# A two-layer decoder trunk: six more pairs of gate blocks and the third SwiGLU's later up blocks as seven half products, and compressed scores as three products per pair of heads

## The chip, the cores and the metric

The kernel runs on one core of a Trainium2 chip. The metric is the device time of one execution in microseconds (us). Three runs of the kernel before took 2000.01, 2000.32 and 2001.31 us; their median is 2000.32.

## The reference

The input is one sequence of 512 tokens with 1024 features, in float32. Two macaron layers follow each other; each adds half a SwiGLU, a mixer and half a second SwiGLU to the stream. The first mixer is an mLSTM. After it one shared set of keys and values is made, among them 31 compressed keys per key head. The second mixer is sparse attention with 16 query heads and 4 key heads; one of its three branches scores each query against the compressed keys.

```python
def swiglu(h, w_in, w_out):
    a, b = jnp.split(h @ w_in, 2, axis=-1)
    return (jax.nn.silu(a) * b) @ w_out
# in a layer, four times in all (D_MODEL = 1024, D_FF = 2816):
h = h + 0.5 * swiglu(rmsnorm(h, g), w_in, w_out)
# in nsa_mixer, per block of 64 queries:
s_c = jnp.einsum('bqhgd,bchd->bqhgc', qq, k_cmp)
p_c = masked_softmax(s_c, ...)
```

## The kernel before

The stream is kept transposed: eight tiles `h` of 128 features x 512 tokens. Every float32 factor of a product is split into a rounded part `hi` and the rest `lo`, and a product of two is three matmuls, hi·hi, lo·hi and hi·lo (`mm3`, L216 to L220). All matmuls are issued at L214. A split is one ScalarE copy (`hi`, L223) and one VectorE subtraction (`lo`, L224); for plain weight blocks the same two stand at L158 and L159.

**Stages.** They run in this order: `ffn0`, `mlstm`, `ffn1`, `kv`, `ffn2`, `nsa`, `ffn3`. The last steps of `kv` (the compressed keys and values, `compress`) are woven into the start of `ffn2`, the third SwiGLU.

**A SwiGLU** (`ffn`, from L337) has 22 gate blocks and 22 up blocks of 128 columns. A plain block multiplies its eight weight strips with the eight tiles of x: 24 matmuls with 512 columns. The blocks run in groups. After a group, its gated products `ghi`, `glo` are multiplied with the group's rows of `w_out` into the eight blocks of the output, two blocks at a time, and each is added to `h`. A group whose product still lacks the norm's factor r is folded: the output is multiplied with r in one VectorE instruction (L515) and added with a second (L516). In the last group r is multiplied into the up block (L362) instead, and the output needs one (L512).

**By seven.** In SwiGLUs 0, 1 and 3 (`SEVEN`) the up blocks from the third on are computed in pairs: with the features cut in two, the tokens cut in two and two blocks of columns, a pair is a 2x2 product of halves, which is done with seven products (Winograd's form of Strassen's method) where eight would do. `by_seven` (L389) issues 7 products x 4 strips x 3 = 84 matmuls with 256 columns. The price is paid elsewhere. Four quarters of the two weight blocks are fetched (`fetch`, L164), VectorE makes four sums of them (`add_quarters`, L173), seven quarters are split (`load_forms`), `x_forms` (L374) makes the sums of x once per SwiGLU, and five VectorE instructions and one ScalarE copy put the results together (L412 to L432). The list `GATES` names the pairs of gate blocks that go the same way: 6, 8, 10, 12, 14, 16 and 20. The groups are 0 to 7, 8 to 15 and 16 to 21 (`EVENS`). In `ffn2` every block is plain, and its groups are 0 to 7, 8 to 14 and 15 to 21 (`THIRDS`).

**The order of the loads.** A dry pass writes down every weight in the order of use; `load_weight` then works that list ahead of the use: up to `ahead` weights (2, or 3 in `SEVEN`) beyond the one wanted. A `fetch` or an `add` in the list is done when the list reaches it. Four buffers hold split weights (`whi`, `wlo`), two hold raw ones. Loads are issued by SyncE, in order. Within the dependencies the framework's scheduler decides each engine's order.

**Scores against compressed keys.** `project_q(b)` makes the queries of two heads, 64 rows each. For each head ScalarE and VectorE write hi and lo into one half of a tile of 128 rows (L1014, L1015) and SyncE copies them to the other half (L1017): four DMAs per pair. A compressed key tile holds hi in its upper and lo in its lower 64 rows, so a head's scores are two matmuls per 128 tokens; `compressed(b)` issues 4 x 2 x 2 = 16 with 32 columns.

Of the kernel before, what the change touches and what calls it, by code (L numbers as in the profile page):

```python
# [19 lines left out]
P = 128  # L20
# [11 lines left out]
GATES = (6, 8, 10, 12, 14, 16, 20)  # L32
# [64 lines left out]
class Net:  # L97
    def __init__(self, ctx, tc, a, order=None):
# [11 lines left out]
        self.fp = None  # L110
        self.ahead = 2
# [51 lines left out]
    def fetch(self, *at):  # L163
# [9 lines left out]
    def add_quarters(self, *at):  # L173

        q = self.raws[at]
        s = self.sums[at] = [None] + [self.fp.tile([P, 512], F32, name=f"s{j}", tag=f"s{j}", bufs=1) for j in range(1, 5)]
# [160 lines left out]
    def ffn(self, i, r=None):  # L337
        nc, tc = self.nc, self.tc
        seven = i in SEVEN
        self.ahead = 3 if seven else 2  # L340
        TT, STT = nc.vector.tensor_tensor, nc.vector.scalar_tensor_tensor
        N = T // 2
        with ExitStack() as ctx:
            pp = ctx.enter_context(tc.tile_pool(name=f"fps{i}", bufs=8 if seven else 6, space=PSUM, reuse_waits="tile"))
            gp = ctx.enter_context(tc.tile_pool(name=f"fg{i}", bufs=8, reuse_waits="tile"))
            self.fp = gp

            nc.vector.memset(gp.tile([P, 96], F32, name="home", tag="home", bufs=1)[:, :1], 0.0)
# [9 lines left out]
            def gate(t, u):  # L358

                if k1 == FB:  # L360
                    v = gp.tile([P, T], F32, name="fd", tag="fd", bufs=2)
                    TT(v, u, r, op=ALU.mult)  # L362
                    u = v
                TT(t, t, u, op=ALU.mult)
                hi = gp.tile([P, T], F32R, name="ghi", tag="ghi")
                lo = gp.tile([P, T], F32R, name="glo", tag="glo")
# [6 lines left out]
            def x_forms(k):  # L373
# [4 lines left out]
                one, two = (gp.tile([P, 3 * N], F32, name="fw", tag="fw", bufs=2) for _ in range(2))  # L378
# [11 lines left out]

            def by_seven(p):
# [35 lines left out]
                TT(two(u1), W[:, :2, :], two(Z), op=ALU.add)  # L427
# [41 lines left out]
            for k0, k1 in EVENS if seven else THIRDS:  # L469
                gs = []  # L470
                for p in range(k0, k1, 2) if seven else range(k0, k1):
                    if seven and p:
                        if p in GATES:
                            ts = [silu(t) for t in (yield from by_seven(p))]
                        else:
                            ts = []
                            for j in range(2):
                                w = self.weight("ffn_in", i, p + j)
                                pa = ps_mm()
# [15 lines left out]
                for m in range(0, KB, 2):  # L495
# [8 lines left out]
                    for k, j in order:  # L504
                        self.mm3(po[j], self.strip(w2[j], k), gs[k], k == 0, k == n - 1)
                        yield
# [851 lines left out]
```

## Time and profile before

One execution was profiled: it took 2000.02 us, its span (first to last instruction) is 1998.2 us.

| engine | busy, us | share of the span |
|---|---|---|
| PE (matmuls) | 1984.4 | 99% |
| PEld (weight loads) | 1715.8 | 86% |
| DVE (VectorE) | 1462.7 | 73% |
| ACT (ScalarE) | 954.4 | 48% |
| POOL (GpSimd) | 166.0 | 8% |

PE is TensorE; its matmuls overlap one another, so a matmul's own duration is longer than the distance to the next one, and what a matmul costs is read from the distance of their starts. L214 is line 214 of the kernel; a name such as `pmm<-xhi,whi` gives the output tile and the inputs. The granted clock of TensorE was full (1.0) in all slices.

### The profile page before, as it was taken

Reading aid. Unit: us, or ns where it says so; the run is one execution under the profiler, and the core shown is the slowest. Engines: PE = TensorE matmul, PEld = TensorE weight load, DVE = VectorE, ACT = ScalarE, POOL = GpSimd, SP = SyncE. Lnnn points to the kernel's source line nnn. Section 1 sums busy time; section 2 is a strip of 40 time slices with the busy share of each in tenths; the row PEclk is TensorE's granted clock in tenths of the full one; section 3 lists DMA queues with packets and bytes.
Section 4 is the critical chain, followed back from the end, with each engine's and each line's share of the span. In section 5 each row is a group of like instructions: output and inputs, shape, how many; then the busy total and the mean of one; then the engine's idle time right before and its main releaser. Section 6 shows DMA issues by size and latency. Waiting matters only on the chain.

```text
span 1998.2 us, 29540 instructions
## 1 busy us (share of the span) xinstructions
PE 1984.4 (99%) x11330; PEld 1715.8 (86%) x11330; DVE 1462.7 (73%) x2604; ACT 954.4 (48%) x1752; POOL 166.0 (8%) x216
## 2 busy tenths in 40 slices
PE   9999999999999999999999999999999999999999
PEld 7989999788778999898888888888778778999898
DVE  8959878757897789686656544445788888769785
ACT  6425334445654345254444322234888865435242
POOL 0000000012200000000101000001444420000000
PEclk9999999999999999999999999999999999999999
DMA  5423422323232323313334332323121132323322
GB/s 189 121 89 103 125 75 65 115 83 95 64 122 90 114 78 111 100 54 116 105 108 123 110 98 87 111 89 105 44 54 43 43 101 80 110 85 101 112 63 90
DMA packets 71469, 188.46 MB, mean 94 GB/s; under 512 B 8480, under 2 KB 9376, under 8 KB 71328
## 3 DMA queue, kind: packets, MB, share of 16 engines
q1 hardware_dynamic: 69936, 183.82, 30.6%
q8 instruction: 89, 1.46, 0.3%
q10 hardware_dynamic: 1008, 1.70, 0.2%
q0 software_dynamic: 384, 1.05, 0.2%
q14 instruction: 52, 0.43, 0.1%
HBM read 177.10 MB, written 2.10 MB: 90 GB/s over the span
## 4 chain that ended last, share of the span: by engine, by line
PE 91%; DVE 3%; ACT 3%; DMA 2%; issue 1%; POOL 0%; SPq 0%; DVEq 0%; ACTq 0%; POOLq 0%
PE pmm L214 80%; PE S L214 3%; PE po L214 2%; PE vps L214 2%; PE pt L1129 1%; DMA q<-in_ffn_in 1%; PE paux L214 1%; ACT pr L1097 1%; PE pn L214 1%; DVE wlo L159 0%; DMA wraw<-in_ffn_in 0%; ACT pth L223 0%; PE pt L214 0%; PE dm L214 0%; PE pg L214 0%
## 5 line engine op out<-in xcount | busy, mean ns | idle before, releaser
L214 PE MATMUL pmm<-xhi,whi 128*128 128x512 f32 (+2 forms) x1468 | 512.2, 349 | 1.4 <-DVE h L1167 0.9
L214 PE MATMUL pmm<-xhi,wlo 128*128 128x512 f32 (+2 forms) x1468 | 508.5, 347 | 0.9 <-DVE wlo L159 0.9
L214 PE MATMUL pmm<-xlo,whi 128*128 128x512 f32 (+2 forms) x1468 | 508.4, 346 | 0.7 <-DVE xlo L267 0.5
L158 ACT ACTIVATE whi<-wraw 128x1024 fp32r<-128x1024 f32 (+3 forms) x296 | 252.1, 867 | 480.4 <-PE pmm L214 360.4
L159 DVE TENSOR_TENSOR wlo<-wraw,whi 128x1024 fp32r<-128x1024 f32 (+3 forms) x296 | 296.4, 1012 | 68.9 <-ACT whi L158 66.0
L214 PEld LDWEIGHTS pmm<-xhi,wlo 128*128 128x128 f32 (+1 forms) x1468 | 277.7, 189 | 34.9 <-DVE wlo L159 1.3
L214 PEld LDWEIGHTS pmm<-xhi,whi 128*128 128x128 f32 (+1 forms) x1468 | 278.0, 189 | 33.0 <-ACT xhi L266 1.6
L214 PEld LDWEIGHTS pmm<-xlo,whi 128*128 128x128 f32 (+1 forms) x1468 | 278.0, 189 | 32.4 <-DVE xlo L267 2.1
L214 PE MATMUL pmm<-ghi,whi 128*128 128x512 f32 x704 | 274.2, 389 | 0.0
L214 PE MATMUL pmm<-glo,whi 128*128 128x512 f32 x704 | 274.0, 389 | 0.0
L214 PE MATMUL pmm<-ghi,wlo 128*128 128x512 f32 x704 | 273.9, 389 | 0.0
L214 PE MATMUL pmm<-thi,whi 128*128 128x256 f32 x816 | 230.9, 283 | 0.0
L214 PE MATMUL pmm<-tlo,whi 128*128 128x256 f32 x816 | 230.9, 283 | 0.0
L214 PE MATMUL pmm<-thi,wlo 128*128 128x256 f32 x816 | 230.9, 283 | 0.0
L223 ACT ACTIVATE whi<-s 128x512 fp32r<-128x512 f32 x204 | 123.0, 626 | 175.1 <-PE pmm L214 112.1
L214 PEld LDWEIGHTS pmm<-thi,whi 128*128 128x128 f32 x816 | 156.7, 192 | 0.0
L214 PEld LDWEIGHTS pmm<-tlo,whi 128*128 128x128 f32 x816 | 156.7, 192 | 0.0
L214 PEld LDWEIGHTS pmm<-thi,wlo 128*128 128x128 f32 x816 | 156.7, 192 | 0.0
L223 ACT ACTIVATE whi<-q 128x512 fp32r<-128x512 f32 x153 | 95.9, 627 | 125.4 <-PE pmm L214 96.1
L214 PEld LDWEIGHTS pmm<-ghi,wlo 128*128 128x128 f32 x704 | 132.1, 188 | 27.5
L214 PEld LDWEIGHTS pmm<-ghi,whi 128*128 128x128 f32 x704 | 132.2, 188 | 27.2
L214 PEld LDWEIGHTS pmm<-glo,whi 128*128 128x128 f32 x704 | 132.2, 188 | 27.1
(341 smaller groups left out, 3120.9 us busy)
## 6 DMA issues: line engine op xcount, KB each, us to landing
q<-in_ffn_in SPq DMA_DIRECT2D x204, 256.0 KB, 2.8
wraw<-in_ffn_in SPq DMA_DIRECT2D x73, 512.0 KB, 3.6
wraw<-in_ffn_out SPq DMA_DIRECT2D x56, 512.0 KB, 3.6
wraw<-in_ffn_out SPq DMA_DIRECT2D x24, 384.0 KB, 3.1
wraw<-in_ffn_out SPq DMA_DIRECT2D x16, 448.0 KB, 3.4
wraw<-in_m_qk SPq DMA_DIRECT2D x8, 512.0 KB, 3.6
wraw<-in_m_v SPq DMA_DIRECT2D x8, 512.0 KB, 3.5
wraw<-in_m_og SPq DMA_DIRECT2D x8, 512.0 KB, 3.6
```

Source lines behind the costliest of these rows:

```text
L158: nc.scalar.activation(hi[:p, c], raw[:p, c], AF.Copy)
L159: nc.vector.tensor_tensor(lo[:p, c], raw[:p, c], hi[:p, c].bitcast(F32), op=ALU.subtract)
L214: self.nc.tensor.matmul(out, lhsT, rhs, start=start, stop=stop)
L223: self.nc.scalar.activation(hi, src, AF.Copy)
L1097: nc.scalar.activation(s, S[:, i, :n], AF.Exp, bias=nx[:, i:i + 1], scale=cc, accum_out=z[:, i:i + 1])
L1129: nc.tensor.transpose(pt[:, col:col + P], pr[br][:, ROW[tb] + sb * P:ROW[tb] + sb * P + P], self.ident)
```

## The change

- `GATES` becomes 4, 6, 8, 10, 12, 14, 16, 18, 20: in SwiGLUs 0, 1 and 3 the pairs 4 and 18 of gate blocks go by seven too.
- The third SwiGLU (`ffn2`) has four groups, 0 to 7, 8 to 11, 12 to 15 and 16 to 21 (`LATER`). In the last three the gate blocks stay plain and the up blocks go by seven. Only the first group is folded; the others multiply r into the up block. The sums of x are made by a new `x_forms_late`, from the tiles of x, in the second half of the first group's output product. The tiles come from pools opened where `compress` had its own; before block 8 the SwiGLU's pool of tiles is closed and another opened (`room`). Quarters and one of the sums have a single buffer there (`qbufs`), `W` too.
- In `by_seven` the first result u1 stays in `W`, and the third sum of quarters overwrites the quarter q[2,1].
- The compressed keys are two tiles, hi and lo, with the two heads of a pair side by side as 2 x 32 columns, each in its own 64 rows with zeros in the others. `project_q` splits both heads' queries at once (`N[b]`), `compressed` issues 4 x 3 = 12 matmuls with 64 columns, and SyncE fills all four head tiles from `N[b]`: eight DMAs per pair.

```diff
-GATES = (6, 8, 10, 12, 14, 16, 20)
+GATES = (4, 6, 8, 10, 12, 14, 16, 18, 20)
+
+LATER = ((0, 8), (8, 12), (12, 16), (16, 22))
...
-                t = q[a, b] = self.fp.tile([P, 512], F32, name=f"q{a}{b}", tag=f"q{a}{b}", bufs=2)
+                t = q[a, b] = self.fp.tile([P, 512], F32, name=f"q{a}{b}", tag=f"q{a}{b}", bufs=self.qbufs)
...
+        s = self.sums[at] = {j: self.fp.tile([P, 512], F32, name=f"s{j}", tag=f"s{j}", bufs=1) for j in (1, 2, 4)}
+        s[3] = q[2, 1]
...
+        self.qbufs = 2 if seven else 1
...
-                if k1 == FB:
-                    v = gp.tile([P, T], F32, name="fd", tag="fd", bufs=2)
+                if not fold:
+                    v = gp.tile([P, T], F32, name="fd", tag="fd", bufs=2) if i == 2 and not k0 else u
                     TT(v, u, r, op=ALU.mult)
...
+            def x_forms_late(k):
+
+                one = sums.tile([P, T], F32, name="tw", tag="tw", bufs=1)
+                two = sums.tile([P, 3 * N], F32, name="tv", tag="tv", bufs=1)
+                (hi1, lo1), (hi2, lo2) = ([t.bitcast(F32) for t in x[b]] for b in (k, k + 4))
+                c = [two[:, N * j:N * j + N] for j in range(3)]
+                TT(one, hi1, lo1, op=ALU.add)
+
+                TT(one[:, :N], one[:, N:], one[:, :N], op=ALU.subtract)
+                for t, half, other in (c[0], slice(N, T), one[:, :N]), (c[1], slice(N, T), one[:, N:]), (c[2], slice(N), c[0]):
+                    TT(t, hi2[:, half], other, op=ALU.subtract)
+                    TT(t, t, lo2[:, half], op=ALU.add)
+                hi = tp.tile([P, 4 * N], F32R, name="thi", tag="thi", bufs=4)
+                lo = tp.tile([P, 4 * N], F32R, name="tlo", tag="tlo", bufs=4)
+                self.split(one[:, :N], hi[:, :N], lo[:, :N])
+                self.split(two, hi[:, N:], lo[:, N:])
+                xt.append((hi, lo))
...
-                W = gp.tile([P, 3, N], F32, name="fw", tag="fw", bufs=2)
+                W = gp.tile([P, 3, N], F32, name="fw", tag="fw", bufs=1 if i == 2 else 3)
-                u1, u2 = (gp.tile([P, T], F32, name="fu", tag="fu", bufs=4) for _ in range(2))
+                u1, u2 = W[:, :2, :].rearrange("p c n -> p (c n)"), gp.tile([P, T], F32, name="fu", tag="fu", bufs=self.qbufs)
...
-            for k0, k1 in EVENS if seven else THIRDS:
-                gs = []
-                for p in range(k0, k1, 2) if seven else range(k0, k1):
-                    if seven and p:
-                        if p in GATES:
+            for k0, k1 in EVENS if seven else LATER:
+                gs, fold = [], k1 < FB if seven else not k0
+                if not seven and k0 == LATER[1][0]:
+                    brief.close()
+                    room("fg2b", 32)
+                    self.ahead = 3
+                for p in range(k0, k1, 2) if seven or k0 else range(k0, k1):
+                    if p and (seven or k0):
+                        if seven and p in GATES:
                             ts = [silu(t) for t in (yield from by_seven(p))]
                         else:
                             ts = []
                             for j in range(2):
+                                if not seven and j == 0 and p != LATER[1][0]:
+                                    self.plan("fetch", i, FB + p)
                                 w = self.weight("ffn_in", i, p + j)
+                                if not seven and (j == 0) == (p != LATER[1][0]):
+                                    if j:
+                                        self.plan("fetch", i, FB + p)
+                                    self.plan("add", i, FB + p)
...
+                        if not seven and not k0 and m >= 4 and t % 8 == 0:
...
+                            x_forms_late((m - 4) + t // 8)
                         self.mm3(po[j], self.strip(w2[j], k), gs[k], k == 0, k == n - 1)
...
+                N[b] = hi, lo = [mp.tile([P, T], F32R, name=n, tag="qn", bufs=3) for n in ("nh", "nl")]
+                self.split(qs, hi, lo)
                 for j in range(2):
-                    s, e = slice(64 * j, 64 * j + 64), slice(64 - 64 * j, 128 - 64 * j)
-                    hi = mp.tile([P, T], F32R, name="qh", tag="q", bufs=8)
-                    lo = mp.tile([P, T], F32R, name="ql", tag="q", bufs=8)
-                    nc.scalar.activation(hi[s], qs[s], AF.Copy)
-                    TT(lo[s], qs[s], hi[s].bitcast(F32), op=ALU.subtract)
-                    for t in (hi, lo):
-                        nc.sync.dma_start(t[e].bitcast(F32), t[s].bitcast(F32))
-                    Q[2 * b + j] = (hi, lo)
+                    Q[2 * b + j] = [mp.tile([P, T], F32R, name=n, tag="q", bufs=8) for n in ("qh", "ql")]
+                    for t, n in zip(Q[2 * b + j], N[b]):
+                        for e in range(2):
+                            nc.sync.dma_start(t[64 * e:64 * e + 64].bitcast(F32), n[64 * j:64 * j + 64].bitcast(F32))
...
-                    for j in range(2):
-                        for part in range(2):
-                            self.mm(Sc[:, tb, j, :], Q[2 * b + j][part][:, tb * P:(tb + 1) * P], self.KC[:, b // 2, :],
-                                    tb + j + part == 0, False)
+                    for n, part in enumerate(((0, 0), (1, 0), (0, 1))):
+                        self.mm(Sc[:, tb].rearrange("p h c -> p (h c)"), N[b][part[0]][:, tb * P:(tb + 1) * P],
+                                self.KC[part[1]][:, b // 2].rearrange("p h c -> p (h c)"), tb + n == 0, False)
```

## Rows read from the trace of the kernel before

**Rows 1.** The page: its first line, the busy time of the engines, and the granted clock of TensorE in 40 slices.

```profile
span 1998.2 us, 29540 instructions
PE 1984.4 (99%) x11330; PEld 1715.8 (86%) x11330; DVE 1462.7 (73%) x2604; ACT 954.4 (48%) x1752; POOL 166.0 (8%) x216
...
PEclk9999999999999999999999999999999999999999
```

**Rows 2.** Busy time of each engine in stretches: most of SwiGLU 0, the end of the third SwiGLU's first output product, the 11 us after it, the rest of the third SwiGLU, the attention.

```profile
core 0: us, PE busy (x) PEld busy (x) DVE busy (x) ACT busy (x) POOL busy (x), PEclk, DMA share, GB/s
33.00:341.00 308.00, 308.00 (x2035) 284.47 (x2034) 253.82 (x419) 136.78 (x220) 2.09 (x2) 1.00 0.31 94
1122.00:1156.00 34.00, 34.00 (x152) 28.14 (x151) 20.13 (x25) 9.25 (x10) 0.00 (x0) 1.00 0.38 113
1156.00:1167.00 11.00, 11.00 (x50) 9.13 (x49) 4.44 (x5) 2.65 (x3) 0.00 (x0) 1.00 0.36 114
1156.00:1397.00 241.00, 241.00 (x1069) 198.09 (x1068) 113.42 (x147) 74.44 (x94) 6.08 (x6) 1.00 0.32 97
1397.00:1622.00 225.00, 222.28 (x1384) 177.03 (x1382) 184.13 (x486) 190.63 (x514) 93.06 (x144) 1.00 0.17 45
```

**Rows 3.** Matmuls in order of time (start, duration): the first and the last of 54 in a row with 512 columns, and of 103 in a row with 256.

```profile
99.76 0.39 PE L214 MATMUL pmm<-ghi,whi 128*128 128x512 f32 x1
...
111.78 0.39 PE L214 MATMUL pmm<-ghi,wlo 128*128 128x512 f32 x1
...
79.74 0.28 PE L214 MATMUL pmm<-thi,whi 128*128 128x256 f32 x1
...
91.98 0.28 PE L214 MATMUL pmm<-thi,whi 128*128 128x256 f32 x1
```

**Rows 4.** VectorE in order of time in the third pair by seven of SwiGLU 0's second group, and the first matmul of that pair's up blocks (PE).

```profile
185.68 0.68 DVE L178 TENSOR_TENSOR s<-q,q 128x512 f32<-128x512 f32 x1
186.28 0.68 DVE L180 TENSOR_TENSOR s<-q,q 128x512 f32<-128x512 f32 x1
...
187.49 0.69 DVE L224 TENSOR_TENSOR wlo<-q,whi 128x512 fp32r<-128x512 f32 x1
...
189.29 0.42 DVE L417 TENSOR_TENSOR fq<-pmm,fw 128x256 f32<-128x256 f32 x1
189.62 0.69 DVE L224 TENSOR_TENSOR wlo<-s,whi 128x512 fp32r<-128x512 f32 x1
...
190.96 0.28 PE L214 MATMUL pmm<-xhi,whi 128*128 128x256 f32 x1
```

**Rows 5.** The same one pair later (the fourth and last of the group): the split of the first form of the up blocks, and the matmul that uses it.

```profile
208.71 0.71 DVE L224 TENSOR_TENSOR wlo<-q,whi 128x512 fp32r<-128x512 f32 x1
...
211.12 0.28 PE L214 MATMUL pmm<-xhi,whi 128*128 128x256 f32 x1
```

**Rows 6.** The end of SwiGLU 0's third group: VectorE (in brackets its idle time and what ended it), ScalarE's splits of the last two gated products, the first matmul of the output product and the 26th, which is the first to read the fifth `glo`.

```profile
321.92 0.69 DVE L420 TENSOR_TENSOR fw<-fq,pmm 128x512 f32<-128x512 f32 x1 [0.78 <-PE pmm L214]
...
324.80 0.69 DVE L427 TENSOR_TENSOR fu<-fw,pmm 128x512 f32<-128x512 f32 x1 [0.78 <-PE pmm L214]
...
330.09 1.29 DVE L224 TENSOR_TENSOR glo<-ft,ghi 128x512 fp32r<-128x512 f32 x2
...
328.73 1.24 ACT L223 ACTIVATE ghi<-ft 128x512 fp32r<-128x512 f32 x2 [1.01 <-DVE ft L364]
...
326.04 0.40 PE L214 MATMUL pmm<-ghi,whi 128*128 128x512 f32 x1
...
331.73 0.39 PE L214 MATMUL pmm<-glo,whi 128*128 128x512 f32 x1
```

**Rows 7.** Groups of instructions by shape (count, busy us, mean ns): the largest split of the sums of x in SwiGLUs 0, 1 and 3, and the two instructions that split a plain block of 512 KB.

```profile
L224 DVE TENSOR_TENSOR tlo<-fw,thi 128x768 fp32r<-128x768 f32 x12 | 11.4, 954 | 1.2 <-ACT thi L223 1.2
...
L159 DVE TENSOR_TENSOR wlo<-wraw,whi 128x1024 fp32r<-128x1024 f32 x145 | 179.7, 1240 | 30.5 <-ACT whi L158 29.7
...
L158 ACT ACTIVATE whi<-wraw 128x1024 fp32r<-128x1024 f32 x145 | 153.3, 1060 | 293.3 <-PE pmm L214 212.6 <-DMA wraw<-in_ffn_out 49.0 <-issue 15.4
```

**Rows 8.** DMA issues: line or tile, engine, count, KB each, median us to landing; and the piece of the chain of waits in which the four quarters for the second SwiGLU's first pair arrive.

```profile
q<-in_ffn_in SPq DMA_DIRECT2D x204, 256.0 KB, 2.8
wraw<-in_ffn_in SPq DMA_DIRECT2D x73, 512.0 KB, 3.6
...
569.70 5.64 DMA q<-in_ffn_in
```

**Rows 9.** The attention: two of the matmuls against compressed keys with ten between them, one of SyncE's issues, the first matmul of the first head's own scores, and the groups of the scores and of the half splits.

```profile
1401.39 0.26 PE L214 MATMUL S<-KC,qh 128*128 128x32 f32 x1
...
1402.62 0.26 PE L214 MATMUL S<-KC,ql 128*128 128x32 f32 x1
...
1402.78 0.47 PE L214 MATMUL S<-K,qh 128*128 128x512 f32 x1
...
1396.39 0.55 SPq L1017 DMA_DIRECT2D ql<-ql  x1
...
L214 PE MATMUL S<-KC,ql 128*128 128x32 f32 x64 | 14.4, 256 | 0.0
...
L1015 DVE TENSOR_TENSOR ql<-qs,qh 64x512 fp32r<-64x512 f32 x16 | 11.7, 734 | 0.7 <-ACT qh L1014 0.4
...
L1014 ACT ACTIVATE qh<-qs 64x512 fp32r<-64x512 f32 x16 | 10.1, 631 | 0.2
```

More of the change, by code (lines that the diff above doesn't have):

```diff
@@ L110, in __init__ @@
         self.fp = None
+        self.compressed = False
         self.ahead = 2
@@ L364, in gate @@
                 TT(t, t, u, op=ALU.mult)
-                hi = gp.tile([P, T], F32R, name="ghi", tag="ghi")
-                lo = gp.tile([P, T], F32R, name="glo", tag="glo")
+                bufs = 8 if seven or not k0 else 6
+                hi = gp.tile([P, T], F32R, name="ghi", tag="ghi", bufs=bufs)
+                lo = gp.tile([P, T], F32R, name="glo", tag="glo", bufs=bufs)
                 self.split(t, hi, lo)
@@ L376, in x_forms @@
                 g1, g2 = (self.g[:, G_FFN + i * KB + b:G_FFN + i * KB + b + 1] for b in (k, k + 4))
-                one, two = (gp.tile([P, 3 * N], F32, name="fw", tag="fw", bufs=2) for _ in range(2))
+                one, two = (gp.tile([P, 3 * N], F32, name="fw", tag="fw", bufs=3) for _ in range(2))
                 h2, c = self.h[k + 4], [two[:, N * j:N * j + N] for j in range(3)]
@@ L425, in by_seven @@
                 yield from product(Z[:, :N], a12, 2)
-                TT(two(u1), W[:, :2, :], two(Z), op=ALU.add)
+                TT(W[:, :2, :], W[:, :2, :], two(Z), op=ALU.add)
                 a22 = self.weight("form", i, p, 3)[0]
@@ L503, in ffn @@
                         order.sort()
-                    for k, j in order:
+                    for t, (k, j) in enumerate(order):
+                        if not seven and not k0 and m >= 4 and t % 8 == 0:
+                            if m == 4 and t == 0:
+                                assert self.compressed
+                                right = dict(bufs=1, side="right", reuse_waits="tile")
+                                tp = ctx.enter_context(tc.tile_pool(name="ft2", **right))
+                                brief = ExitStack()
+                                sums = brief.enter_context(tc.tile_pool(name="ft2s", **right))
+                            x_forms_late((m - 4) + t // 8)
                         self.mm3(po[j], self.strip(w2[j], k), gs[k], k == 0, k == n - 1)
@@ L510, in ffn @@
                         for c in (slice(0, T // 2), slice(T // 2, T)) if last else (slice(0, T),):
[L511 removed]
+                            if not fold:
                                 STT(h[:, c], po[j][:, c], 0.5, h[:, c], op0=ALU.mult, op1=ALU.add)
@@ L825, in kv @@
         self.V = [kvp.tile([P, 2 * KVH, 2 * HD], F32R, name=f"V{tb}") for tb in range(NTB)]
-        self.KC = kvp.tile([P, KVH, CW], F32R, name="KC")
+        self.KC = [kvp.tile([P, KVH, 2, CW], F32R, name=f"KC{part}") for part in range(2)]
         self.VC = kvp.tile([P, KVH, 2, 2 * HD], F32R, name="VC")
@@ L911, in compress @@
             late.close()
+            self.compressed = True
         with ExitStack() as ctx:
```

25 lines of the change are left out of this document (16 added, 9 removed).

## The prediction

> **What bounds the kernel now.** I read the page first, then the busy time by stretches, then the order of time of single engines. The page has TensorE (PE) busy for 99% of the span at full granted clock [rows 1]; since matmuls overlap, that alone proves little. The stretches are better: in SwiGLU 0 and in the third SwiGLU PE is busy for every microsecond, with VectorE at 82% in the one and 47% in the other [rows 2]. The order of time settles it. 54 matmuls with 512 columns start (111.78 - 99.76) / 53 = 0.2268 us apart, 103 with 256 columns (91.98 - 79.74) / 102 = 0.1200 us apart [rows 3], and the SwiGLUs run at these distances throughout. There the time is the number of matmuls times their distance, as long as split weights and gated products are ready in time. The attention is different: PE 222 of 225 us, but ScalarE 191 and VectorE 184 [rows 2]; there engines take turns, and a matmul saved is not always a microsecond saved.
>
> **The sum's own time.** The profiled execution took 2000.0 us, 1.8 of it outside the span [rows 1]; the median of the runs, 2000.3, is the same within what follows. A difference under 0.2% (4 us) can't be told from none in this kernel.
>
> **A pair by seven.** Plain, a pair is 2 x 24 = 48 matmuls x 0.2268 = 10.88 us; by seven it is 84 x 0.1200 = 10.08. That saves 0.80 us. The change makes 6 more such pairs in SwiGLUs 0, 1 and 3 (4 and 18 in each) and 7 in the third: 13 x 0.80 = 10.4 us of matmuls, 4.8 in the three and 5.6 in the third. The output products keep their 528 matmuls, however the groups are cut, since the group sizes add up to 22 blocks either way.
>
> The Trainium skill, in "TensorE: Matmul & The Clock Gate" (Back-to-back issue gap), gives an isolated matmul N / 2.4 + 2.5 ns: 216 ns with 512 columns and 109 with 256. By that a pair would save 48 x 0.2158 - 84 x 0.1092 = 1.19 us, and the 13 pairs 15.4, which would bring the forecast below to 1985.8. The rows lie 11 ns above it at both sizes; the sum goes by the rows.
>
> **SwiGLUs 0, 1 and 3: VectorE.** Back to back its 512-column instructions start 0.60 us apart (186.28 - 185.68) and a 256-column one takes 0.33 (189.62 - 189.29) [rows 4]. One unit by seven needs 4 sums + 7 splits (6.6 us) and 2 x 0.60 + 3 x 0.33 (2.2) to put results together: 8.8. A gate and an up unit, with two silu factors and two gates (2 x 0.60 + 4 x 0.60), make 21.2 us against 20.16 of PE. So in a row of such pairs VectorE falls back 1.1 us per pair. The trace shows it: the first form of the up blocks is ready 190.96 - 188.18 = 2.78 us ahead of its matmul in the second group's third pair [rows 4], and 211.12 - 209.42 = 1.70 in the fourth [rows 5]. Group two is not changed. The first group gets two such pairs in a row, fewer than the four that group two stands. The third group gets three, 16, 18 and 20, and there r is multiplied in too, 2 x 0.60 per pair. Lead in its last pair: the 2.78 of group two's third pair less 2 x 1.2 = 0.4 us. Still positive. At the end of that group the fifth `glo` now is ready at 330.09 + 0.69 = 330.78, 0.95 us before its matmul at 331.73, and VectorE waited for PE twice for 0.78 us in the last unit [rows 6]. The extra pair costs it 1.1 + 1.2 = 2.3; 1.56 of that goes into these waits, 0.74 into the 0.95. Nothing is left to lose, so I take 0.3 us per SwiGLU; the bounds are 0 and 2.3. Net: 4.8 - 0.9 = 3.9 us. Keeping u1 in `W` and the third sum in a quarter moves no work; the second makes one sum wait for another on the same engine.
>
> **The third SwiGLU.** 5.6 us come off PE. Three things are new.
>
> First, `x_forms_late`: per tile pair one add of 0.60, seven of 0.33, and splits of 0.33 and 0.95 [rows 4, 7], 4.2 us, so 17 for four. Then four sums (2.4) and two splits (1.2) before the first unit by seven: 20.5 us of VectorE. It idles 34.0 - 20.1 = 13.9 us in the stretch before block 8 and 11.0 - 4.4 = 6.6 in its two plain blocks, 20.4 in all [rows 2]. That just fits if the scheduler draws the sums forward. If it keeps them to the last 22 us of the output product, about a third of the 13.9 is lost. I take 1.0 us, bounds 0 and 4.
>
> Second, groups of four. In the third group of SwiGLU 0 the fifth `ghi` is ready at 328.73 + 0.62, 3.3 us after the output product's first matmul at 326.04, and the `glo` at 4.7 [rows 6]. With six blocks the matmul wants it at 5.7. With four blocks the last two products are the third and the fourth, wanted after 12 and 13 matmuls, 2.7 and 2.9 us. PE so waits 0.6 us (the `ghi` alone) to 1.8 (the `glo` in the same chain), unless the scheduler lets later matmuls pass. VectorE is less busy here than there, so I take 1.0 for each of two groups, 2.0 us; bounds 0 and 3.6.
>
> Third, single buffers. A pair's quarters can be fetched only when the previous unit's last form is split, which waits for a weight buffer until that unit begins. What hides it is the unit itself, 10.08 us: the last split is done about 1.4 us into it (0.6 and 0.7 on the two engines [rows 4, 9]), the last quarter takes 2.8 and the next plain block's 512 KB, behind it on SyncE, 3.6 [rows 8]: 7.8, and its two splits 1.06 + 1.24 [rows 7]: 10.1. That is just in time, with three quarters loaded earlier, and with slack if the scheduler issues the block's load, which has little to wait for, ahead of the last quarter. I cost it at nothing; what it costs without that cover is a rival below.
>
> The other groups' outputs: two of them are no longer folded, which spares VectorE an instruction per output block; it is not the bound there. Net: 5.6 - 3.0 = 2.6 us.
>
> **The attention.** Scores against compressed keys go from 16 to 12 matmuls per pair of heads, 32 fewer in all. With 32 columns they start (1402.62 - 1401.39) / 11 = 0.112 us apart [rows 9], nearly as far as 256-column ones [rows 3], so 64 columns cost no more: 32 x 0.112 = 3.6 us off PE. ScalarE and VectorE lose one half split each per pair (16 of 0.63 and 0.73 become 8 [rows 9]). These scores no longer wait for the copies. Against that, SyncE issues eight copies per pair at 0.55 us each instead of four [rows 9]: 2.2 us more before the last tile lands. For all pairs but the first two heads' worth of work lies between; for the first, whose own scores start right after the compressed ones at 1402.78 [rows 9], it can be late. Bounds: a gain of 6 (all of it, and the two other engines' relief) and a loss of 2.2. Since PE isn't the only bound there, I take three quarters of 3.6, 2.7 us.
>
> **Sum.** 2000.0 - 3.9 - 2.6 - 2.7 = 1990.8 us.
>
> **The rivals.**
>
> *The attention gives nothing* (chance 0.13). The waits on ScalarE and GpSimd stay, or the copies come late: 1990.8 + 2.7 = 1993.5. For it: ScalarE at 85% [rows 2]. Against: the relief of ScalarE itself.
> The Trainium skill ("DMA: Bandwidth & Descriptors", Rules for kernel authors) advises against two transfers to disjoint partition halves, since they serialize on the same engines; the change makes just such pairs. No row of before shows two at once.
>
> *VectorE becomes the bound in the last groups of SwiGLUs 0, 1 and 3* (0.12). If a chain is slower than my two differences of leads, each loses the full 2.3 us: 3 x 2.0 more, 1996.8.
>
> *The single buffers in the third SwiGLU starve PE* (0.08; the slower side). If all four quarters wait for the last split, 1.4 + 5.6 (four quarters together [rows 8]) + 3.6 + 2.3 for both splits = 12.9 us against 10.08. The four pairs that follow another one in their group (10, 14, 18, 20) then start 2.8 us late, and 4 us if two sums of quarters (2 x 0.6) come first in VectorE's order. 4 x 2.8 = 11.2 gives 2002.0, 4 x 4 = 16 gives 2006.8. It decides from 9.2 / 4 = 2.3 us per pair: from there on the change gains nothing. For it: one buffer, and a queue in order. Against: three of the four quarters are free earlier.
>
> *More comes through* (0.07): no stall anywhere and the attention's full 3.6: 2000.0 - 4.8 - 5.6 - 3.6 = 1986.0, or less.
>
> That the change doesn't do what it says is hardly open: the counts of matmuls will tell.
>
> **How the numbers follow.** The forecast holds 0.60 of the chance, with its own range 1987.5 to 1994. The range for 8 in 10 reaches down to the case of more, 1985, and up past the second rival to 1998. Faster by over 0.2% means under 1996.3: the forecast, the first rival, the case of more and half of the second, 0.86. Within 0.2%: the other half and a part of the third, 0.09. Slower: the rest of the third, 0.05.
>
> **What would show it.** Matmuls with 256 columns: 51 x 84 = 4284 become 64 x 84 = 5376, still 0.120 us apart; those with keys KC 128 become 96, still about 0.112 apart. In the third SwiGLU, gaps of 0.6 to 1.8 us at the start of two output products, and one of about 1 us before its first unit by seven. In SwiGLUs 0, 1 and 3 leads of about 0.4 us in pair 20. I am wrong if PE stands still between units of the third SwiGLU, if VectorE shows no idle time in the third groups while PE waits for `wlo`, or if the attention is longer than 225 us.

## The result and the profile after

The changed kernel takes 1989.02 us (median of four runs, 1988.38 to 1989.33) against 2000.82 for the kernel before on the same chips (four runs, 2000.01 to 2001.37): a ratio of 0.994, with an interval of 0.9926 to 0.9955. That is 11.8 us less. I had forecast 1990.8, which was 9.5 us under the 2000.3 then known: the direction and most of the size came out. The time is 1.8 us lower than I said and, since the kernel before took 0.5 us more beside it, the gain 2.3 us larger.

The page of the changed kernel's profile, the lines that answer to [rows 1]:

```profile
span 1986.6 us, 31009 instructions
PE 1972.6 (99%) x11766; PEld 1725.8 (87%) x11766; DVE 1558.3 (78%) x2836; ACT 985.8 (50%) x1838; POOL 161.7 (8%) x218
...
PEclk9999999999999999999999999999999999999999
```

The span is 11.6 us shorter, and the busy time of TensorE (PE) 11.8, although there are 436 more matmuls. VectorE (DVE) has 96 us more work. The same stretches as in [rows 2], moved to where they now lie:

```profile
core 0: us, PE busy (x) PEld busy (x) DVE busy (x) ACT busy (x) POOL busy (x), PEclk, DMA share, GB/s
33.00:341.00 308.00, 307.05 (x2108) 286.72 (x2108) 265.60 (x447) 139.93 (x231) 1.79 (x2) 1.00 0.31 94
1114.00:1149.00 35.00, 35.00 (x174) 29.15 (x173) 29.77 (x51) 12.33 (x16) 0.00 (x0) 1.00 0.31 96
1149.00:1160.00 11.00, 11.00 (x50) 9.13 (x49) 5.33 (x11) 1.48 (x2) 0.00 (x0) 1.00 0.39 135
1149.00:1383.00 234.00, 234.00 (x1311) 205.29 (x1309) 161.06 (x254) 91.96 (x142) 5.65 (x6) 1.00 0.33 100
1383.00:1608.00 225.00, 221.75 (x1349) 173.07 (x1348) 181.35 (x488) 187.04 (x507) 88.65 (x144) 1.00 0.25 66
```

In the third SwiGLU VectorE went from 47% to 69%, and PE is still busy in every microsecond. Before block 8 (the second line) VectorE has 29.8 us of work in 35, where it had 20.1 in 34.

To see where the time came from I cut both executions at the same matmuls and took the distances of their starts (us, worked out from all matmuls of the two traces):

```
stretch                                                  before   after   difference
start to the mLSTM's gates (SwiGLU 0)                     358.7   357.8   -0.9
the mLSTM up to its last `dm`                             188.9   188.9    0.0
to the first `paux` (SwiGLU 1)                            392.7   391.1   -1.6
keys and values, third SwiGLU, to the attention           450.5   445.1   -5.4
attention, to the row scale of SwiGLU 3                   277.4   275.3   -2.1
SwiGLU 3 from there                                       325.8   324.2   -1.6
```

The forecast had -3.9 for SwiGLUs 0, 1 and 3 (here -4.1), -2.6 for the third (here -5.4) and -2.7 for the attention (here -2.1). So the one large error is in the third SwiGLU.

### The profile page after: what moved, and what is told of

The parts are those of the page before. It is cut to its first block, busy times and chain, and to the rows that moved or that the text cites. A ratio compares the mean times of both kernels' runs of the same rounds, so it can differ in the third digit from the quotient of the medians.

```text
span 1986.6 us, 31009 instructions
## 1 busy us (share of the span) xinstructions
PE 1972.6 (99%) x11766; PEld 1725.8 (87%) x11766; DVE 1558.3 (78%) x2836; ACT 985.8 (50%) x1838; POOL 161.7 (8%) x218
## 4 chain that ended last, share of the span: by engine, by line
PE 91%; ACT 3%; DVE 3%; DMA 1%; issue 1%; POOL 0%; SPq 0%; DVEq 0%; ACTq 0%
PE pmm L218 81%; PE S L218 2%; PE vps L218 2%; PE po L218 2%; ACT pr L1151 1%; PE paux L218 1%; PE pt L1183 1%; PE pn L218 1%; DVE wlo L162 1%; ACT pth L227 1%; PE pt L218 0%; PE dm L218 0%; ACT nx L1148 0%; DMA q<-in_ffn_in 0%; ACT whi L161 0%
## 5 line engine op out<-in xcount | busy, mean ns | idle before, releaser
L218 PE MATMUL pmm<-xhi,whi 128*128 128x256 f32 (+2 forms) x1416 | 475.1, 336 | 0.7 <-ACT whi L161 0.5
L218 PE MATMUL pmm<-xlo,whi 128*128 128x256 f32 (+2 forms) x1416 | 471.3, 333 | 1.1 <-DVE xlo L271 1.1
L218 PE MATMUL pmm<-xhi,wlo 128*128 128x256 f32 (+2 forms) x1416 | 471.4, 333 | 0.6 <-DVE wlo L162 0.6
L161 ACT ACTIVATE whi<-wraw 128x1024 fp32r<-128x1024 f32 (+5 forms) x278 | 225.8, 829 | 360.2 <-PE pmm L218 239.0
L162 DVE TENSOR_TENSOR wlo<-wraw,whi 128x1024 fp32r<-128x1024 f32 (+5 forms) x278 | 266.1, 968 | 79.3 <-ACT whi L161 78.2
L218 PE MATMUL pmm<-tlo,whi 128*128 128x256 f32 x1024 | 289.8, 283 | 0.0
L218 PE MATMUL pmm<-thi,wlo 128*128 128x256 f32 x1024 | 289.7, 283 | 0.0
L218 PE MATMUL pmm<-thi,whi 128*128 128x256 f32 x1024 | 289.6, 283 | 0.0
L227 ACT ACTIVATE whi<-q 128x512 fp32r<-128x512 f32 x256 | 159.2, 624 | 123.6 <-PE pmm L218 108.7
L228 DVE TENSOR_TENSOR wlo<-q,whi 128x512 fp32r<-128x512 f32 x256 | 177.3, 693 | 14.4 <-ACT whi L227 14.1
```

Source lines behind the costliest of these rows:

```text
L161: nc.scalar.activation(hi[:p, c], raw[:p, c], AF.Copy)
L162: nc.vector.tensor_tensor(lo[:p, c], raw[:p, c], hi[:p, c].bitcast(F32), op=ALU.subtract)
L218: self.nc.tensor.matmul(out, lhsT, rhs, start=start, stop=stop)
L227: self.nc.scalar.activation(hi, src, AF.Copy)
L228: self.nc.vector.tensor_tensor(lo, src, hi.bitcast(F32), op=ALU.subtract)
```

## The experiments

Times are medians; the kernel before ran beside each group of runs, at 2000.7 to 2000.9 us.

### The three parts, each alone

The first kernel is the one before with only the longer list of gate pairs and the places for u1 and the third sum that it needs:

```diff
-GATES = (6, 8, 10, 12, 14, 16, 20)
+GATES = (4, 6, 8, 10, 12, 14, 16, 18, 20)
```

> Only the first part: pairs 4 and 18 of gate blocks by seven in SwiGLUs 0, 1 and 3, with u1 kept in W and the third sum in a quarter; the third SwiGLU and the attention are those of before. Theory (a pair is worth 0.80 us as long as VectorE's lead stays above zero): six pairs, 4.8 us at most, and 3.9 as the stages of the whole change showed (0.9, 1.4, 1.6), so about 4 us under the kernel before. Rival (VectorE's third groups eat the pairs): 2 us or less.

Measured: 1996.94 us, a ratio of 0.9979 (0.997 to 0.9988), so 3.8 us less.

The second is the changed kernel with the old `GATES` and the old attention, so that only the third SwiGLU is new.

```diff
-GATES = (4, 6, 8, 10, 12, 14, 16, 18, 20)
+GATES = (6, 8, 10, 12, 14, 16, 20)
...
-                    for n, part in enumerate(((0, 0), (1, 0), (0, 1))):
+                    for j in range(2):
+                        for part in range(2):
```

> Only the second part: the third SwiGLU's up blocks by seven in groups of 8, 4, 4 and 6; GATES and the attention are those of before. Theory (nothing waits there): 5.2 to 5.6 us under the kernel before. My forecast with its two waits at the groups of four and one before the first unit: 2.6 us.

Measured: 1995.97 us, 0.9975 (0.9966 to 0.9984), 4.8 us less. The stretch with the third SwiGLU takes 445.0 us in its profile, as in the changed kernel. In that one execution the first stretch is 3.1 us longer than before (361.8): PE stands 2.29 us ahead of the matmuls with `rc`, where it had stood 1.10. The program is the same at that place, but the scheduler has put these eight behind 130 matmuls instead of 124. The profiled execution is the slowest of the eleven (1997.64); the last section comes back to it.

The third is the kernel before with only the twelve matmuls of compressed scores and their eight copies:

```diff
-                    for j in range(2):
-                        for part in range(2):
+                    for n, part in enumerate(((0, 0), (1, 0), (0, 1))):
```

> Only the third part: compressed scores in three products per pair of heads, with eight copies. Theory: about 2.1 us under the kernel before, as the stage in the whole change showed. If the parts are independent the three add up to the whole change's 11.6 to 11.8 us; rival: a part works only with another, and the sum is off by more than 1.5 us.

Measured: 1998.89 us, 0.999 (0.9981 to 0.9999), 1.9 us less.

The three parts alone make 10.5 us, the whole 11.8. The interval of each part is some 1.8 us to either side, so a difference of 1.3 us lies within the noise, and no part is seen to need another for its gain. The gate pairs stand as I had them (3.9), the attention is under, the third SwiGLU far over.

### The output products of four blocks, in order

My forecast had PE wait twice for the last `ghi` and `glo` of a group of four. In the changed kernel's trace there is no such wait: the whole of this part of the program is one piece of PE in the chain of waits (start, us, what, number of instructions).

```profile
1119.07 264.03 PE pmm L218 x1440
```

The order of time shows why. PE at the start of the first of these output products, and VectorE beside it:

```profile
1196.28 0.39 PE L218 MATMUL pmm<-ghi,whi 128*128 128x512 f32 x1
...
1199.01 0.84 PE L218 MATMUL pmm<-ghi,whi 128*128 128x512 f32 x3
1199.69 0.63 PE L218 MATMUL pmm<-glo,whi 128*128 128x512 f32 x2
...
1201.09 0.87 PE L218 MATMUL pmm<-ghi,whi 128*128 128x512 f32 x3
...
1198.98 0.69 DVE L228 TENSOR_TENSOR glo<-ft,ghi 128x512 fp32r<-128x512 f32 x1
...
1200.97 0.69 DVE L228 TENSOR_TENSOR glo<-ft,ghi 128x512 fp32r<-128x512 f32 x1 [0.70 <-ACT ghi L227]
```

The first four products run in the regular change of `ghi,whi`, `glo,whi`, `ghi,wlo`. From 1199.01 on there are three `ghi,whi` in a row and two `glo,whi`: matmuls of other products have been put ahead of the one whose `glo` is done only at 1198.98 + 0.69 = 1199.67. The last `glo`, done at 1201.66, is passed in the same way. To test this I pinned the matmuls of these two output products to the order of the program and left all else.

```diff
-        self.nc.tensor.matmul(out, lhsT, rhs, start=start, stop=stop)
+        ins = self.nc.tensor.matmul(out, lhsT, rhs, start=start, stop=stop)
+        if self.pin:
+            self.tc.keep_in_program_order(ins)
...
+                        self.pin = i == 2 and n == 4
                         self.mm3(po[j], self.strip(w2[j], k), gs[k], k == 0, k == n - 1)
+                        self.pin = False
```

> The changed kernel, with the matmuls of the two output products of the groups of four kept in the order of the program, so that no later matmul passes one that waits. Theory (the wait for the last gated products is real and hidden by passing): 0.6 to 1.8 us more per group, 1.2 to 3.6 us more than the changed kernel. Rival (the gated products come in time anyway): no difference, under 0.4 us.

Measured: 1991.88 us, 0.9952 (0.994 to 0.9965), 2.9 us more than the changed kernel; the stretch with the third SwiGLU has 447.4 us instead of 445.1. The view of waits for PE over the two groups (us in total, times, longest), and PE where the first two fall:

```profile
PE pmm L219 <- DVE glo L231: 1.1, 4, 0.3
```

```profile
1200.79 0.39 PE L219 MATMUL pmm<-ghi,whi 128*128 128x512 f32 x1
1201.50 0.50 PE L219 MATMUL pmm<-glo,whi 128*128 128x512 f32 x1 [0.32 <-DVE glo L231]
...
1202.77 0.49 PE L219 MATMUL pmm<-ghi,whi 128*128 128x512 f32 x1
1203.50 0.50 PE L219 MATMUL pmm<-glo,whi 128*128 128x512 f32 x1 [0.23 <-DVE glo L231]
```

Four times the next matmul starts 0.71 to 0.73 us after the one before instead of 0.23, which is 4 x 0.49 = 2.0 us; the profile books only 1.1 of it as waiting, since it counts from the modelled end of the matmul before. The matmul behind each of the four also starts 0.11 us late, which makes up the 2.3 of the stretch. So the wait that I had costed at 2.0 us is real, and in the changed kernel it is hidden by the order of the matmuls.

### Has VectorE anything left in SwiGLUs 0, 1 and 3?

I had found VectorE at the edge in the third groups and taken 0.3 us per SwiGLU for it. The trace of the changed kernel has a lead of 0.9 us in the last pair: the split of the second form of the up blocks, and the first matmul of the product that uses it.

```profile
314.81 0.71 DVE L228 TENSOR_TENSOR wlo<-s,whi 128x512 fp32r<-128x512 f32 x1
...
316.46 0.28 PE L218 MATMUL pmm<-thi,whi 128*128 128x256 f32 x1
```

316.46 - (314.81 + 0.71) = 0.94 us; SwiGLUs 1 and 3 have the same at their ends, and 1.94 in the fourth pair of the second group. The first form, for which I had forecast 0.4, leads by 1.9, since VectorE now splits it ahead of three of the four sums:

```profile
312.41 0.71 DVE L228 TENSOR_TENSOR wlo<-q,whi 128x512 fp32r<-128x512 f32 x1
313.01 0.71 DVE L183 TENSOR_TENSOR s<-s,q 128x512 f32<-128x512 f32 x1
...
315.02 0.28 PE L218 MATMUL pmm<-xhi,whi 128*128 128x256 f32 x1
```

To see whether the 0.94 are the real margin, I gave VectorE more to do.

```diff
                 if not fold:
+                    if seven:
+                        TT(gp.tile([P, T], F32, name="fx", tag="fx", bufs=1), u, r, op=ALU.mult)
```

> The changed kernel with one more VectorE multiply of 128 x 512 (0.60 us) for each up block in SwiGLUs 1, 2 and 4 (counted from one), into a tile that nothing reads: 1.2 us more per pair by seven, everywhere. My forecast's theory has VectorE at the edge there: a row of three or four such pairs falls back by another 3.6 to 4.8 us against leads of 0.9 to 1.9 us, so PE waits 2 to 3 us per group of that kind, 6 to 15 us in all. Rival, there is slack that the leads don't show, because the scheduler lets other matmuls pass and VectorE makes up the rest in the output products: under 2 us.

The edit acts only where r is multiplied in before the output product, that is in the third group of each of these SwiGLUs (counted from 0 in this document: 0, 1 and 3), and not "everywhere" as the expectation says; so 1.2 us per pair, in three pairs each. Measured: 1996.51 us, 0.9977 (0.9968 to 0.9986), 7.5 us more than the changed kernel. The three places, in SwiGLUs 0, 1 and 3, and what VectorE did ahead of the first:

```profile
317.73 0.39 PE L218 MATMUL pmm<-xhi,wlo 128*128 128x256 f32 x1 [1.27 <-DVE wlo L228]
...
894.86 0.39 PE L218 MATMUL pmm<-xhi,wlo 128*128 128x256 f32 x1 [2.41 <-DVE wlo L228]
...
1946.97 0.39 PE L218 MATMUL pmm<-xhi,wlo 128*128 128x256 f32 x1 [1.30 <-DVE wlo L228]
...
316.40 0.67 DVE L185 TENSOR_TENSOR s<-q,s 128x512 f32<-128x512 f32 x1
317.01 0.67 DVE L228 TENSOR_TENSOR wlo<-q,whi 128x512 fp32r<-128x512 f32 x1
```

PE there starts 1.55, 2.69 and 1.58 us after the matmul before, where 0.12 is usual: so 1.4, 2.6 and 1.5 us are lost, 5.5 together. Two pairs stand ahead of each place with 2 x 1.2 = 2.4 us of additional work. So VectorE is near its edge in these groups, as the theory had it. That the margin is 0.94 is not shown: PE waits here for the first form and not for the second, because in this run VectorE splits it behind all four sums. 2.4 less 0.94 is 1.5, but that two of the three places lose as much is no test of that lead. Of the other 2.0 us of the 7.5, 0.5 are not in the profiled execution, which took 7.0 us more than the profiled one of the changed kernel; the median is that of executions with a lower granted clock (see the last section). Most of what is left lies ahead of 35 us, where single executions of the changed kernel and its variants differ by as much.

### The attention: matmuls or copies?

The attention gained 2.1 us where 32 matmuls at 0.112 would be 3.6. The first test puts those matmuls back in another form: a fourth product, of the two low parts, so 128 instead of 96.

```diff
-                    for n, part in enumerate(((0, 0), (1, 0), (0, 1))):
+                    for n, part in enumerate(((0, 0), (1, 0), (0, 1), (1, 1))):
```

> The changed kernel with a fourth product of low parts per pair of heads in the compressed scores, so 128 matmuls against compressed keys as before the change, 64 columns each, all else (the copies, the split of both heads at once) kept. If the attention's gain is the matmuls taken away, this loses it again: 32 x 0.11 = 3.5 us if PE bounds each of these places, about 2.1 if only as much counts as the attention gained. Rival, the gain came from one split for two heads and from the scores no longer waiting for copies: less than 1 us longer.

Measured: 1992.9 us, 0.9961 (0.9949 to 0.9974), 3.9 us more than the changed kernel. The matmuls count in full, at 3.9 / 32 = 0.12 us each. The second test makes the copies later.

```diff
+                spare = mp.tile([P, 2, 96], F32R, name="qx", tag="qx", bufs=1)
+                for n in range(4):
+                    e = slice(64 * (n % 2), 64 * (n % 2) + 64)
+                    nc.sync.dma_start(spare[e, n // 2, :].bitcast(F32), N[b][n // 2][e, :96].bitcast(F32))
```

> The changed kernel with four small copies more per pair of heads, 64 partitions x 96 words, issued on SyncE ahead of the eight real ones, into a tile that nothing reads. They add about 4 x 0.6 = 2.4 us before the last real copy of each pair lands, 8 times. If the attention's missing 1.5 us went into the first pair's copies landing late, this adds at least 1.0 us, and up to 2.4 if only the first pair has no cover; if every pair lacks cover it adds some 10. Rival, the copies are hidden everywhere and the missing part lies in engines that take turns: under 0.5 us.

Measured: 1988.46 us, 0.994 (0.9927 to 0.9952): no difference from the changed kernel. SyncE's queue (SPq) at the first pair of heads in that run, and PE at the same time:

```profile
1387.20 1.11 SPq L1072 DMA_DIRECT2D qx<-nh  x2
...
1393.65 1.23 SPq L1077 DMA_DIRECT2D ql<-nl  x2
...
1395.30 0.40 PE L218 MATMUL S<-K,qh 128*128 128x512 f32 x1
1395.54 0.40 PE L218 MATMUL pmm<-xhi,whi 128*128 128x512 f32 x1
...
1396.24 0.50 PE L218 MATMUL S<-K,ql 128*128 128x512 f32 x1
```

The last real copies are issued at 1393.65 there, and at 1390.27 in the changed kernel. `S<-K,ql` followed its `qh` matmul by 0.23 us in the changed kernel and follows here by 0.94, but matmuls of a projection have moved in between. So the copies are not what ate the missing 1.5 us.

The distances of starts, summed by tile over the stretch of the attention, say more. Behind the products with `KC` 12.9 us became 10.3. That is 2.6 and not 3.6: in a row the 64-column products are 0.112 us apart, like the 32-column ones, but in the kernel before 17 of the 128 were followed after only 0.03 us, and I had counted 0.112 for all. All other matmuls went from 219.7 to 221.4 up to the last product with `V`, so the attention itself gained 0.9 us. The other 1.2 us lie behind it, 1.1 of them at the first matmul of SwiGLU 3. There the kernel before stands:

```profile
1645.42 0.39 PE L214 MATMUL pmm<-ohi,wlo 128*128 128x512 f32 x1
1646.71 0.47 PE L214 MATMUL pmm<-xhi,whi 128*128 128x512 f32 x1 [0.90 <-DVE h L1167]
```

In the changed kernel the same two matmuls start 0.23 us apart (1636.68 and 1636.91). The wait for VectorE is in all three traces with the old attention (1.29 us, and 0.77 and 0.79 in the first and second experiment, from start to start) and in none with the new one; why is not traced. The run with the fourth product says what the rest of the change in the attention does. It has as many products with `KC` as the old attention, and the stretch takes 279.6 us in its trace, against 276.7 to 277.4 with the old one. So 32 matmuls fewer are worth 3.9 us, and the rest of the change takes 2 to 3 us of that back. Which wait between the engines that is stays open.

### One pair more

If two SwiGLUs are bound by their matmuls, a tenth pair by seven should give 0.80 us in each.

```diff
+        gates = GATES + (2,) if i in (1, 3) else GATES
```

> The changed kernel with one more pair by seven, pair 2, in the second and fourth SwiGLU, so ten pairs there instead of nine. If these two are bound by the number and distance of matmuls alone, as the changed kernel's stages say, each gains 0.80 us: 1.6 us less, about 1987.4. Rival, VectorE is late: pair 2 is the first by seven of the stage, and its forms would have to be ready behind the first plain blocks' splits; PE then waits before its unit, with a lead below zero there, and the time is the same or up to 2 us longer. If the margin of the first group was already used, the wait shows in pair 4 instead.

Measured: 1991.64 us, 0.9954 (0.994 to 0.9968), 2.6 us more than the changed kernel. My rival named the wrong tile. The split forms of pair 2's weights are ready (the shortest lead is 5.4 us in both SwiGLUs), and PE stands before the matmuls that spread the row scale `rc` over the partitions, 2.03 us in SwiGLU 1 and 2.02 in SwiGLU 3. The view of waits for PE (600 to 640 us), and a piece of VectorE's order of time:

```profile
PE pmm L218 <- DVE rc L307: 1.6, 1, 1.6
```

```profile
606.09 0.15 DVE L307 SCALAR_TENSOR_TENSOR rc<-rq,rc 128x4 f32<-128x4 f32 x1
606.16 0.95 DVE L228 TENSOR_TENSOR tlo<-fw,thi 128x768 fp32r<-128x768 f32 x1
607.03 0.68 DVE L228 TENSOR_TENSOR wlo<-s,whi 128x512 fp32r<-128x512 f32 x1
607.64 0.68 DVE L228 TENSOR_TENSOR wlo<-q,whi 128x512 fp32r<-128x512 f32 x1
608.24 0.15 DVE L305 TENSOR_TENSOR rq<-rc 128x4 f32<-128x4 f32 x1
```

`rc` comes out of twelve small instructions of 0.15 us, each of which needs the one before. Pair 2 by seven brings the forms of x and of the weights into the same time, and the scheduler puts them between: 2.15 us from the start of one link to that of the next here. The chain takes 7.0 us there (603.36 to 610.33) and 4.9 in the changed kernel.

Two runs followed from this. In the changed kernel SwiGLU 0 has a wait of the same kind, 1.27 us. The first run issues the spreading matmuls later in the program.

```diff
-                    if p == 1 and t == KB + 6 and r is None:
-                        rows.append(self.rstd_rows(columns[0], ps_mm()))
...
+                if p == 1 and r is None:
+                    rows.append(self.rstd_rows(columns[0], ps_mm()))
```

> The changed kernel with the eight small matmuls that spread the row scale rc over the partitions issued behind the second plain pair's last strip instead of two strips ahead of it. In the changed kernel's trace TensorE stands 1.27 us ahead of them in the first SwiGLU, waiting for the last of a row of twelve small VectorE instructions that the forms of x are put between. Two strips are 6 x 0.2268 = 1.36 us of matmuls that need no rc. If that gap is on the path, it goes: 1.2 us less, about 1987.8. Rival, r is then 1.4 us later for the silu factors of both plain pairs, and what follows is late by as much: no difference, or up to 1 us more.

Measured: 1989.35 us, 0.9943 (0.993 to 0.9955): no difference. The gap is still there, 1.25 us:

```profile
32.89 0.39 PE L218 MATMUL pmm<-xhi,wlo 128*128 128x512 f32 x1
34.13 1.16 PE L218 MATMUL pmm<-cst,rc 128*128 128x128 f32 x8 [0.86 <-DVE rc L307]
```

The run says nothing for or against my reason: the order of PE's matmuls in SwiGLU 0 is the same in both kernels, since the scheduler had already put these eight behind the second plain pair's last strip. The second run has pair 2 by seven and the later spreading, and takes the chain earlier in SwiGLUs 1 and 3, where the sums for it are ready by 594 us (SwiGLU 1), 6 us ahead of their use.

```diff
-                    if p == 1 and t == 3 and r is None:
+                    if (p, t) == ((0, 13) if i in (1, 3) else (1, 3)) and r is None:
```

> The kernel with pair 2 by seven in the second and fourth SwiGLU, with rc spread behind the second plain pair, and in these two SwiGLUs the sums for rc taken three strips ahead of the first plain pair's end, some 2.7 us earlier. Its trace without that showed TensorE standing 2.03 and 2.02 us ahead of rc's matmuls there and 1.47 in the first SwiGLU. If pair 2 itself costs nothing more, all three gaps go and the 2 x 0.80 us of the two pairs come through: 1989.0 - 1.6 - 1.2 = 1986.2. Rival, the forms of x for pair 2 are the limit, and the wait only moves from rc to the pair's first forms: within 1 us of the changed kernel.

Measured: 1987.23 us (1986.63 to 1988.61), 0.9933 (0.9919 to 0.9946). In SwiGLU 1 `rc` is done at 606.72, 3.9 us ahead of its matmuls at 610.64, and no gap is left there or in SwiGLU 3; the one in SwiGLU 0 (1.38 us) stays.

```profile
606.57 0.15 DVE L307 SCALAR_TENSOR_TENSOR rc<-rq,rc 128x4 f32<-128x4 f32 x1
...
610.64 1.05 PE L218 MATMUL pmm<-cst,rc 128*128 128x128 f32 x8
```

The lead of 3.9 us is more than the 1.4 us by which the spreading moved, so the earlier chain alone would have been enough. The run is 4.4 us better than the kernel with pair 2 alone. By the medians it is also 1.8 us better than the changed kernel, near the 2 x 0.80 that were counted, but that is 0.09% and not shown: in its trace the stretch of SwiGLU 1 takes 390.8 us instead of 391.1, and attention and SwiGLU 3 together take 599.0 instead of 599.5, so 0.8 of the 1.6.

## Why the prediction was right, and where not

**What bounds the kernel.** Right. The time followed the number of matmuls and their distances: 13 pairs x 0.80 = 10.4 us were counted and 5.4 + 4.1 = 9.5 of them arrived. By an estimate from the gap that the Trainium skill gives for an isolated matmul ("TensorE: Matmul & The Clock Gate", Back-to-back issue gap), 1.19 us a pair, the seven of the third SwiGLU would have given 8.3 us. They gave 5.4, so the rows decided rightly.

**SwiGLUs 0, 1 and 3: 4.8 less 0.9.** The sum is right (3.8 alone, 4.1 in the whole), the reason for the 0.9 is not. My lead of 0.4 us for the first form of pair 20 was too small: it is 1.9, since VectorE splits that form earlier than in the trace of before, and the second form is now the closest with 0.94. As the kernel stands nothing is lost there; the run with more work on VectorE shows that little is left. Behind it VectorE is later for the output product, as I had said, but there matmuls pass each other too; PE in SwiGLU 0's third group:

```profile
330.57 0.84 PE L218 MATMUL pmm<-ghi,whi 128*128 128x512 f32 x3
```

Two pairs of 0.80 came in full in SwiGLU 1 and in SwiGLU 3, so VectorE costs nothing there. What is missing is all in SwiGLU 0, where waits ahead of `rc` (1.27 us; 1.0 to 1.1 in the kernel before and in the third experiment) and at a `glo` at 229.35 (0.45 us between starts; ahead of that `glo`, ScalarE had stood 3.4 us for the load of a block of `w_out`) took part of it; I had no step for either. How much, one execution can't tell: in the other traces with the changed kernel's SwiGLU 0, this stretch takes 357.8 to 359.4 us.

**The third SwiGLU: 5.6 less 3.0.** Here the prediction failed. The 5.6 us are right to 0.2. "I take 1.0 us" for the sums of x and the first unit: measured 0. The scheduler did draw the sums forward; their splits lie between 1122 and 1152 us, and the first unit's second form is ready 2.85 us ahead of its matmul. The row of splits on VectorE and the unit's first matmul:

```profile
1163.15 1.29 DVE L228 TENSOR_TENSOR wlo<-s,whi 128x512 fp32r<-128x512 f32 x2
...
1165.25 0.28 PE L218 MATMUL pmm<-xhi,whi 128*128 128x256 f32 x1
```

The first `wlo` of the row, the second form's, is done at 1163.84, and its matmuls begin at 1165.25 + 12 x 0.12 = 1166.69. "I take 1.0 for each of two groups, 2.0 us": the price was right, as the pinned run shows (2.0 us of gaps, 2.3 in the stretch), but I charged it although I had written the condition that removes it, "unless the scheduler lets later matmuls pass". The trace of before could not show it: in none of its output products do two `ghi,whi` start in a row. In the changed kernel they do at five places, the two groups of four and the third groups of SwiGLUs 0, 1 and 3.

**Single buffers.** Costed at nothing, and right: behind the first unit, no unit of the third SwiGLU has a lead under 7.1 us, where I had counted it just in time.

**The attention: three quarters of 3.6.** It is 2.1 in the whole and 1.9 alone, against 2.7. That this is near is luck. The matmuls with `KC` saved 2.6 and not 3.6, since not all of them had stood in a row; the rest of the attention took 1.7 back; and 1.2 came from a wait at the start of SwiGLU 3, for which I had no step. The late copies, which I had named as the risk, are hidden.

**The rivals.** *The attention gives nothing* is out by the time, 1.9 us alone (with an interval of 0.2 to 3.8), though only 0.9 us of the whole arise in the attention itself. The Trainium skill ("DMA: Bandwidth & Descriptors", Rules for kernel authors) advises against two transfers to disjoint partition halves because they serialize. Of that hardly an effect is to be seen here: the copies to two halves of the partitions land in a median of 2.3 to 2.4 us after the change, and the single ones before took 2.2. *VectorE becomes the bound* is out as the kernel stands, but not by much: 2.4 us more work ahead of the last pair cost 1.4 to 2.6 us. *The single buffers starve PE* is out. *More comes through* had half of it: no stall in the third SwiGLU, but not the attention's full 3.6.

**The sum.** Against the 2000.8 us measured beside it, the errors are -2.8 (the third SwiGLU: 3.0 us of waits that did not come, less the 0.2 that its pairs fell short), +0.6 (attention) and -0.2 (the other SwiGLUs). That makes 2.4 us in the traces and 2.6 by the medians; the base of 2000.0 that I used was 0.8 lower, and 1.8 are left.

## What to carry to other kernels

Where one engine is busy throughout and a scheduler orders its instructions, a late operand costs only what no other instruction can fill: before a stall is charged, count the later instructions that are ready and may pass. A small chain of dependent instructions on a busy engine is as long as what is put between its links, so its first link is to be issued as early as its input allows. Adding work to an engine bounds its margin from above; it does not confirm a single lead, because the scheduler may order that engine's work anew, and here the wait moved to another tile.

## What the runs showed of the hardware

In the profiled execution of the second experiment PE stood for 2.29 us up to 35.34 (starts of the last plain matmul and of the first with `rc`), and the granted clock then fell. Windows, the columns as above, and some of the matmuls:

```profile
33.00:35.50 2.50, 0.59 (x3) 0.17 (x3) 2.50 (x11) 1.54 (x3) 0.00 (x0) 1.00 0.89 309
35.50:36.00 0.50, 0.50 (x4) 0.50 (x5) 0.50 (x1) 0.50 (x2) 0.00 (x0) 0.68 0.86 258
36.00:41.00 5.00, 5.00 (x20) 4.18 (x19) 4.87 (x12) 3.56 (x7) 0.00 (x0) 0.69 0.12 46
41.00:46.00 5.00, 5.00 (x24) 4.14 (x23) 3.55 (x6) 3.91 (x6) 0.00 (x0) 1.00 0.00 0
...
35.34 1.79 PE L218 MATMUL pmm<-cst,rc 128*128 128x128 f32 x8 [1.91 <-DVE rc L307]
...
37.79 0.63 PE L218 MATMUL pmm<-xhi,wlo 128*128 128x512 f32 x1
38.21 0.63 PE L218 MATMUL pmm<-xhi,whi 128*128 128x512 f32 x1
```

From 37.36 to 39.07 the 512-column matmuls start 0.43 us apart instead of 0.2268, which is the lower of the two levels (1.2 instead of 2.4 GHz). The first fourteen matmuls behind the stand take 3.98 us to the start of the next, and 2.39 in the kernel before: 1.6 us on top of the stand itself. After the stands of 2.03 us in the run with pair 2 and of 2.69 us in the run with more work on VectorE the clock stayed at 1.00 in the profiled executions, so the length of the stand alone does not decide it. It also differs from one execution of a kernel to the next. Of the eleven of the second experiment, only the profiled one has a mean granted clock of 0.999, and the others 1.000. With more work on VectorE six of ten have 0.999 and take 1996.3 to 1997.1 us; the four with 1.000 take 1994.7 to 1995.9.
